# Three more expert-weight buffers, and 23 weight loads issued by GpSimd, in a fused decoder-layer kernel

## The chip, the cores and the metric

The kernel runs on one core of a Trainium2 chip. Its metric is the device time of one launch, in microseconds (us), lower being better; three runs of the kernel before gave 762.72 us in the median (762.62 to 764.26). Five engines work at once, each with its own in-order queue: TensorE (PE, with its weight loads shown as PEld), VectorE (DVE), ScalarE (ACT), GpSimd (POOL) and SyncE (SP, which here issues most transfers). Transfers run on the 16 DMA engines of the core, whoever issues them.

## The reference

One decoder layer on 512 tokens of width 1024, all in float32. A token mixer with three branches, then a mixture of experts:

```
h = rmsnorm(x, g_mix);  proj = h @ w_in          # q, k, v, indexer, conv, memory query, gate logits
o_a = sparse attention: an indexer picks the top 128 causal keys of each query, 8 heads on 2 key heads
o_b = conformer convolution (GLU, causal depthwise conv of 31, layernorm, swish)
o_m = cross-attention to 256 memory tokens
merged = sum over the branches of sigmoid(gate) * (o_branch @ w_br)
x = x + merged @ w_o
h2 = rmsnorm(x, g_ffn)
group = argmax(h2 @ w_rg + b_rg);  two best experts of that group's 8 by h2 @ w_re + b_re
for n in 32 experts: out += combine[:, n] * ((silu(h2 @ up_a[n]) * (h2 @ up_b[n])) @ w_down[n])
x = x + out
```

The weights of the 32 experts are 32 x 3 MB, read once: they are the largest part of the traffic.

## The kernel before, in words

The program has four stretches. The **mixer** (to about 415 us) computes memory keys, convolution, indexer and attention; its weights are 512 KB chunks `w`, loaded on SP into a ring of three buffers (`raw_w`, L130) and split by ACT and DVE into a high part `wh` (L127) and a low part `wl` (L128), which PE multiplies three ways. The **output projection** (the mark "w_o", to about 490 us) multiplies `merged` by w_o in eight column blocks. The **router** (to about 509 us) computes expert choice, token lists and an order of experts. The **experts** run as 16 windows of two experts each (64 tokens an expert) and one further window for the two busiest experts; PE multiplies the gathered tokens `xt` by the expert weights in `up` (L1167) and `down` (L1181).

The expert weights are cut into 192 chunks `we` of 128 x 1024 floats (512 KB, 4 KB a partition). `seq` lists them in the order of use: the first 44 belong to four pairs that are fixed beforehand (EARLY), the later ones to pairs whose numbers DVE works out at run time (`ordi`, L1047) and SP loads into registers (L749). The chunks go round a ring of 42 buffers: `RINGS` says how many buffers each tag has, and the tags lie in memory that other tiles used before (`ot`, `mg`, `wh`, `wl`, `xc`, `hw`, `hx` are tiles of the mixer and of w_o; `w3`, `w1`, `wg`, `s5` lie in pools opened when the mixer's pools `gp` and `bp` are closed). `fetch` (L773) allocates the next buffers of the ring and issues one load each on SP. A load waits until the readers of whatever lay in its buffer are done: for the first turn these are the mixer, w_o or the router, from the second turn on it is the `up` or `down` that used the chunk 42 places earlier. A loaded chunk stays in its buffer until PE has used it.

The instructions of each engine are put in order by a scheduler when the program is built; a row's place can thus move although its code did not. GpSimd computes reciprocal roots (L146, L889), clears tiles, and issues the gathers of tokens (`xg`, L1001), the scatters of results (`out`, L1158) and the reloads of the busiest pair (L1199). [...]

Of the kernel before, what the change touches and what calls it, by code (L numbers as in the profile page):

```python
# [8 lines left out]
F32 = mybir.dt.float32  # L9
# [11 lines left out]
P = 128  # L21
# [19 lines left out]
NPRE = 4  # L41
# [3 lines left out]
def pair(j):  # L45

    e = (j // EPG) * 2 * EPG + j % EPG
    return e, e + EPG


TURN = list(range(NPRE, NW)) + list(range(NPRE))
# [16 lines left out]
for _name, _w in (("g_mix", KD), ("g_mem", KD), ("b_gate", 24), ("conv_b", 4), ("ln_g", 4), ("ln_b", 4),  # L68
# [9 lines left out]
          + [("rkv", i) for i in range(3)] + [(n, i) for n in ("rqi", "rqa") for i in range(4)])  # L78

RING = 3  # L80
RING_A = 9
RING_B = 6
SPLIT = 3
RINGS = (("w3", RING_B), ("w1", RING_A), ("ot", 4), ("mg", 4), ("w", RING), ("wh", SPLIT), ("wl", SPLIT), ("xc", 2),
         ("hw", 3), ("hx", 2), ("wg", 1), ("s5", 2))
CONV_LOW = 1500
TOPK_LOW = 900

# [1 line left out]
def build(nc, tc, I, O, dbg=None):  # L90
    V, A, G, T, SY = nc.vector, nc.scalar, nc.gpsimd, nc.tensor, nc.sync
    es = ExitStack()
    with es:
        cpool = es.enter_context(tc.tile_pool(name="cpool", bufs=1))
        wpool = es.enter_context(tc.tile_pool(name="wpool", bufs=RING))
        spool = es.enter_context(tc.tile_pool(name="spool", bufs=SPLIT))
        mpool = es.enter_context(tc.tile_pool(name="mpool", bufs=1))
# [10 lines left out]
        hp = es.enter_context(tc.tile_pool(name="hp", bufs=1, side="right"))  # L108
        bp = p1b.enter_context(tc.tile_pool(name="bp", bufs=1, side="right"))
        gp = p1a.enter_context(tc.tile_pool(name="gp", bufs=1))  # L110
# [24 lines left out]
        def split_w(w, n=1024):  # L135
            wh = spool.tile([P, 1024], F32R, name="wh", tag="wh")
            wl = spool.tile([P, 1024], F32R, name="wl", tag="wl")
            split_into(wh[:, :n], wl[:, :n], w[:, :n])
            return wh, wl

        def next_w(*key, n=1024):
            return split_w(raw_w(*key), n)
# [55 lines left out]
            return [[hp.tile([P, 2, S], F32R, name=f"{name}{v}{i}", tag="ot", bufs=4) for i in range(2)] for v in "hl"]  # L198

        conv_w = gp.tile([P, 4 * CW], F32, name="conv_wh")  # L200
        bgate = gp.tile([P, 24], F32, name="bgate")
        lng = gp.tile([P, 8], F32, name="lng")
        gqk = gp.tile([P, 1], F32, name="gqk")
        b_r = cpool.tile([P, 36], F32, name="b_r")
# [48 lines left out]
        for k in range(KD):  # L253
# [14 lines left out]
            wh, wl = split_w(kv_raw[k] if k < RING else raw_w("kv", k))  # L268
# [150 lines left out]
        def gate_unit(b, c):  # L419
            ps = mmt("gate")  # L420
            cm_unit(ps, *next_w("gt", b, c))
            t = g2("gt", "gt")
            A.activation(t, ps, AF.Tanh, scale=0.5, bias=bgate[:, b * 8 + c:b * 8 + c + 1])  # L423
            return t
# [31 lines left out]
        for h in range(MH + 1):  # L456
            if h < MH:
                mem_s1(h)
            if h + 1 < MH:
                qm_unit(h + 1)  # L460
            elif len(gm) < 4:
                gm.append(gate_unit(2, len(gm)))
            if h >= 1:
                mem_s2(h - 1)
            if len(gm) < 4 and h > 0:
                gm.append(gate_unit(2, len(gm)))

        mark("A proj")

# [273 lines left out]
        ea = es.enter_context(tc.tile_pool(name="ea", bufs=1, reuse_waits="tile"))  # L743
        rp = es.enter_context(tc.tile_pool(name="rp", bufs=1, side="right", reuse_waits="tile"))
# [7 lines left out]
        def chunk(e, c):  # L752

            if e in EARLY:
                return I["we"][e, c]
            if e not in at_pos:
                at_pos[e] = expert_at(e)
            return I["we"][bass.ds(at_pos[e], 1), c].rearrange("o p n -> (o p) n")
# [3 lines left out]
        for j, last in zip(TURN + [None], [None] + TURN):  # L762
# [3 lines left out]
                seq += [(e, 4 + f) for f in range(2) for e in pair(last)]  # L766
            if j is not None and j != NW:
                seq += [(e, 3) for e in pair(j)]
        pools = dict(ot=hp, hw=hp, hx=hp, w3=rp, xc=rp, w1=ea, w=wpool, wh=spool, wl=spool, s5=ea, wg=ea, mg=mpool)
        slots = [tag for tag, n in RINGS for _ in range(n)]  # L770
        bufs = {tag: slots.count(tag) for tag in slots}
        fetched, used = [], [0]

        def fetch(count, behind=None):
            for n in range(len(fetched), min(len(fetched) + count, len(seq))):
                tag = slots[n % len(slots)]
                w = pools[tag].tile([P, 1024], F32, name="we", tag=tag, bufs=bufs[tag])
                if behind is not None and tag == "s5":
                    G.tensor_copy(w[:, 0:1], behind[:, 0:1])
                e, c = seq[n]  # L780
                SY.dma_start(w, chunk(e, c))  # L781
                fetched.append(w)

        def expert_raw(e, c):
# [8 lines left out]
        def eat(tag, name, bufs=1, dt=F32):  # L793
            return ea.tile([P, 1024], dt, name=name, tag=tag, bufs=bufs)
# [9 lines left out]
        A.dma_start(gB, I["gf"].to_broadcast([P, D]))  # L804
        out_v = O["out"][0:S, :].rearrange("(t p) d -> p t d", p=P)
        h2d_v = h2d.rearrange("(t p) d -> p t d", p=P)
        fetch(RING_B + RING_A + 4 + 4)
        lg = sct("lg")
        zz = eat("s4a", "zz")
        G.memset(zz[:, 0:148], 0.0)  # L810
        T.matmul(lg[:, 0:148], zz[:, 0:P], zz[:, 0:148], start=True, stop=False)
        lists = pvt("lists")

        def back(c, xs):

            ps = trt()
            for t in range(NT):
                T.transpose(ps[:, t * P:(t + 1) * P], xs[:, t * P:(t + 1) * P], ident)
            ys = eat("s5", "x1t", 2)
            if c < KD - 2:  # L820
                A.activation(xs[:, 512:1024], ps, AF.Square)
                V.reduce_sum(sqs[:, :, c], xs[:, 512:1024].rearrange("p (t d) -> p t d", t=NT), axis=AX.X)
            A.copy(ys[:, 0:512], ps)
            g = gB[:, None, c * P:(c + 1) * P].to_broadcast([P, NT, P])
            V.tensor_mul(ys[:, 512:1024].rearrange("p (t d) -> p t d", t=NT), ps.rearrange("p (t d) -> p t d", t=NT), g)
            y3 = ys.rearrange("p (s t d) -> p s t d", s=2, t=NT)
            (SY if c >= KD - 2 else A).dma_start(h2d_v[:, :, c * P:(c + 1) * P], y3[:, 1])
            A.dma_start(out_v[:, :, c * P:(c + 1) * P], y3[:, 0])
# [14 lines left out]
        for c in range(KD):  # L843
            ps = mmt("wo")
            wh, wl = split_w(wo_raw[c])
            for k in range(KD):
                if c >= 1 and k == 4:
                    back(c - 1, logits(c - 1))
                mm3(ps, wh[:, k * P:(k + 1) * P], wl[:, k * P:(k + 1) * P], mgh[k], mgl[k], k == 0, k == KD - 1)
            xs = eat(("s4a", "s4b")[c % 2], "x1c", 1 + c % 2)  # L850
            V.tensor_add(xs[:, 0:512], ps, X[c // 2][:, c % 2])
            if c >= KD - 2:
                A.activation(xs[:, 512:1024], xs[:, 0:512], AF.Square)
            XS[c] = xs
# [3 lines left out]
        xs = logits(KD - 1)  # L858
# [6 lines left out]
                T.matmul(junk, w, x, start=True, stop=True)  # L865

        busy_pe(5, xs[:, 512:1024])
        fetch(RING + 2 * SPLIT + 2)


        mark("router")
# [18 lines left out]
        _, L = r3("lgs", NT, 36)  # L890
# [6 lines left out]
        _, pr = r3("pr", NT, NG)  # L897
# [13 lines left out]
        _, oh = r3("oh", NT, 2, NE)  # L911
# [15 lines left out]
        _, rk = r3("rk", NT, 2, NE)  # L927
# [40 lines left out]
        first = slot_tokens(lists, ea, "f")  # L968
# [255 lines left out]
        AC, AT = {}, {}  # L1224
        fill(0)
        fill(1)
        fetch(len(slots) - len(fetched), first)
        XT[0] = window_x(0)
        order_experts()
        fill(2)  # L1230
# [32 lines left out]
        def extra_windows(j, sl):  # L1263
            ids = [expert_at(e) for e in pair(j)]
            with tc.For_i(0, S // CAP - 1, 1):
                V.tensor_scalar_add(sl, sl, -float(CAP))
                ps = eq.tile([P, 512], F32, name="lists2", tag="tr", bufs=2)
                rb = eat("wg", "soh16o").bitcast(F16)
                one_hot(rb, sl)
                token_lists(ps, rb)  # L1270
                idx = slot_tokens(ps, ea, "o")
                ro = eat("wg", "soh2")
                ps = eq.tile([P, 512], F32, name="scales2", tag="tr", bufs=2)
                one_hot(ro, sl)
                scale_lists(ps, ro)
                lst = (idx,) + slot_scales(ps, ea, "o")
                gather(j, lst[0])
                xt = window_x(j)
                ps = eq.tile([P, 512], F32, name="up", tag="up", bufs=2)

                def chunks(c):
                    ws = []
                    for e in ids:
                        w = rp.tile([P, 1024], F32, name="w3", tag="w3", bufs=RING_B)
                        SY.dma_start(w, I["we"][bass.ds(e, 1), c].rearrange("o p n -> (o p) n"))
                        ws.append(w)
                    return ws

                for c in range(4):
                    up(xt, c, chunks(c), ps)  # L1290
                at = act_t(activate(ps, lst, j), j)
                yp = [eq.tile([P, 512], F32, name=f"dn{n}", tag="dn", bufs=2) for n in range(2)]
                for f in range(2):
                    down(at, f, chunks(4 + f), yp)
                scatter(j, yp, lst[0])
# [108 lines left out]
```

## Time and profile before

| | before |
|---|---|
| median of 3 runs | 762.72 us |
| the profiled execution | 763.3 us |
| its span, first to last instruction | 761.5 us |
| PE / DVE / ACT / POOL busy | 716.2 / 477.2 / 266.1 / 89.0 us |
| `we` chunks loaded on SP | 192 |
| DMA traffic | 161.14 MB |

The span is what the profile covers; 1.8 us of the execution lie around it. A busy time says how long an engine had an instruction in work. PE's is 94% of the span, but its ends are modelled, so it does not tell alone whether PE or what feeds it sets the pace: that is read by stretch, from the share of the DMA engines, from the waits and from the chain that ended last.

### The profile page before, as it was taken

How to read it: one execution, taken by the hardware profiler on the slowest of the kernel's cores; microseconds unless marked ns; L12 is line 12 of the kernel's file. 1: busy time of each engine (PE TensorE's matmuls, PEld its weight loads, DVE VectorE, ACT ScalarE, POOL GpSimd, SP SyncE). 2: the span in 40 equal slices, each digit the busy share in tenths (PEclk: the TensorE clock that was granted, in tenths of full speed). 3: DMA queues.
4: the chain of work that ended last, by engine and by line, in shares of the span. 5: the costliest groups of instructions: out<-in, count | busy, mean ns of one | idle time of the engine just before them, and what ended most of it. 6: DMA issues, size and time to landing. Idle time of an engine off the chain costs nothing. (4 is left out here: it accounts for less than half of the span.)

```text
span 761.5 us, 10081 instructions
## 1 busy us (share of the span) xinstructions
PE 716.2 (94%) x3468; PEld 478.1 (63%) x3468; DVE 477.2 (63%) x1085; ACT 266.1 (35%) x503; POOL 89.0 (12%) x82
## 2 busy tenths in 40 slices
PE   5999999999999999999999999989999998889882
PEld 4778888897878778888777888744333333233220
DVE  5879989999999999999987944272111112111100
ACT  6732254455633366236775432102111111000100
POOL 1010010011000050000000000021236322100010
PEclk9999999999999999999999999999999999999997
DMA  9642221223222221221212899989999999999982
GB/s 355 214 142 83 85 83 55 74 66 111 83 83 83 83 84 64 104 83 52 89 55 96 325 367 350 355 306 379 380 398 357 357 370 384 363 385 396 390 324 48
DMA packets 56685, 161.14 MB, mean 212 GB/s; under 512 B 9508, under 2 KB 17956, under 8 KB 56624
## 3 DMA queue, kind: packets, MB, share of 16 engines
q1 hardware_dynamic: 42320, 147.74, 51.5%
q0 software_dynamic: 6624, 8.46, 4.8%
q10 hardware_dynamic: 7680, 4.20, 1.9%
q8 instruction: 29, 0.48, 0.2%
q14 instruction: 32, 0.26, 0.1%
HBM read 162.93 MB, written 13.11 MB: 231 GB/s over the span
## 5 line engine op out<-in xcount | busy, mean ns | idle before, releaser
L1167 PE MATMUL up<-we,xt 128*64 128x512 f32 x544 | 140.7, 599 | 5.3 <-DMA we<-in_we 5.1
L127 ACT CAST wh<-w 128x1024 fp32r<-128x1024 f32 (+2 forms) x75 | 78.3, 1045 | 81.1 <-PE proj L315 25.4
L128 DVE TENSOR_TENSOR wl<-w,wh 128x1024 fp32r<-128x1024 f32 (+2 forms) x75 | 90.8, 1212 | 13.1 <-ACT wh L127 12.1
L1167 PEld LDWEIGHTS up<-we,xt 128*64 128x64 f32 x544 | 39.1, 136 | 77.3 <-issue 58.1
L329 DVE SCALAR_TENSOR_TENSOR y<-u,conv_wh,y 128x512 f32<-128x512 f32 x120 | 84.1, 743 | 0.3
L1157 DVE COPY y<-dn 128x512 f32<-128x512 f32 x17 | 11.8, 691 | 108.5 <-PE dn L1181 108.5
L1181 PE MATMUL dn<-we,acth 128*64 128x512 f32 x272 | 73.6, 596 | 0.6 <-issue 0.6
L315 PE MATMUL gate<-h,wh 128*128 128x512 f32 x240 | 68.3, 397 | 0.0
L1156 ACT COPY y<-dn 128x512 f32<-128x512 f32 x17 | 10.0, 586 | 123.4 <-PE dn L1181 72.3
L1181 PEld LDWEIGHTS dn<-we,acth 128*64 128x64 f32 x272 | 24.1, 136 | 44.5 <-issue 36.3
L315 PEld LDWEIGHTS gate<-h,wh 128*128 128x128 f32 x240 | 44.4, 188 | 9.4
L1158 POOL DMA_INDIRECT out<-y,midx x16 | 25.4, 1585 | 138.9 <-DVE y L1157 128.8
L315 PE MATMUL gate<-h,wl 128*128 128x512 f32 x120 | 34.8, 400 | 0.0
L315 PE MATMUL mm<-h,wh 128*128 128x512 f32 x120 | 32.6, 396 | 0.0
L1140 ACT COPY xt<-xtr 128x512 f32<-128x512 f32 x18 | 10.4, 585 | 57.7 <-PE xtr L1139 57.6
L423 ACT ACTIVATE gt<-gate,bgate 128x512 f32<-128x512 f32 x24 | 16.5, 686 | 39.8 <-PE gate L315 39.6
L1175 DVE COPY acth<-atr 128x256 f32<-128x256 f32 x17 | 7.2, 424 | 36.7 <-PE atr L1173 36.7
L1150 DVE SCALAR_TENSOR_TENSOR acts<-up,mwt,acts 128x256 f32<-128x256 f32 x16 | 7.7, 483 | 31.8 <-ACT acts L1149 31.8
L605 DVE MAX8 v<-score 128x8 f32<-128x256 f32 (+2 forms) x48 | 26.5, 556 | 0.8
L606 DVE MATCH_REPLACE8 score<-v,score 128x256 f32<-128x256 f32 (+2 forms) x48 | 26.0, 542 | 0.0
L315 PEld LDWEIGHTS gate<-h,wl 128*128 128x128 f32 x120 | 22.5, 188 | 5.5 <-issue 0.5
L315 PEld LDWEIGHTS mm<-h,wh 128*128 128x128 f32 x120 | 22.4, 187 | 5.2
(400 smaller groups left out, 1452.7 us busy)
## 6 DMA issues: line engine op xcount, KB each, us to landing
we<-in_we SPq DMA_DIRECT2D x192, 512.0 KB, 11.3
w<-in_wp SPq DMA_DIRECT2D x75, 512.0 KB, 3.5
x<-in_x SPq DMA_DIRECT2D x4, 512.0 KB, 8.3
xr<-in_xt SPq DMA_DIRECT2D x4, 512.0 KB, 5.2
out<-x1t ACTq DMA_DIRECT2D x8, 256.0 KB, 5.9
h2d<-x1t ACTq DMA_DIRECT2D x6, 256.0 KB, 8.5
m<-in_memt SPq DMA_DIRECT2D x2, 512.0 KB, 5.8
m<-in_mem SPq DMA_DIRECT2D x2, 512.0 KB, 9.7
```

The costliest lines, as they stand in the source:

```text
L127: A.copy(wh, w)
L128: V.tensor_sub(wl, w, wh.bitcast(F32))
L315: T.matmul(ps, a[:, k * P:(k + 1) * P], b[k], start=(a is wh and b is rh and k == 0), stop=(b is rl and k == n - 1))
L329: V.scalar_tensor_tensor(Y[c], U[c][:, j:j + S], w, Y[c], op0=ALU.mult, op1=ALU.add)
L423: A.activation(t, ps, AF.Tanh, scale=0.5, bias=bgate[:, b * 8 + c:b * 8 + c + 1])
L605: V.max(v8, sel[t])
L606: V.match_replace(sel[t], v8, sel[t], GONE)
L1140: (A.copy if i or j == 0 else V.tensor_copy)(xt[i], ps.bitcast(F32))
L1157: V.tensor_copy(y[:, 512:1024], yp[1])
L1158: G.indirect_dma_start(out=O["out"], out_offset=bass.IndirectOffsetOnAxis(ap=ix[:, col:col + 1], axis=0), in_=y, in_offset=None, bounds_ch ...
L1167: T.matmul(ps[h * CAP:(h + 1) * CAP], xt[k // 4][:, o + h * CAP:o + (h + 1) * CAP], ws[h][:, i * 512:(i + 1) * 512], start=(k == 0), stop= ...
L1181: T.matmul(yp[n][h * CAP:(h + 1) * CAP], at[:, f * P + h * CAP:f * P + (h + 1) * CAP], ws[h][:, n * 512:(n + 1) * 512], start=(f == 0), st ...
```

## The change

The DMA scratch area is set to 4 KB a partition, and three buffers of a new tag `wn` are made in the constants' pool. They take the first three chunks, whose loads are issued on SP in the mixer, ahead of the mark "A proj". The ring is now written as a list `SLOTS` of 45 buffers: `wn` 3, `w3` 6, `w1` 6, `wx` 3 (six and three of the former nine `w1`), then as before. The chunks 4 to 26 are issued by GpSimd; three calls of `fetch` replace one, two tiles of w_o's tail (`s4b`, `s5`) are allocated between them so that `w1` lies where the attention's tiles were, and the loads into `ot` and `mg` are preceded by a one-column copy on GpSimd from the 18th chunk's buffer, so that they come behind it. `fetch(AHEAD)` and the last `fetch` are cut to what is left: 10 chunks and 8. The bias tile `bgate` moves to the constants' pool, and the clearing of `zz` from GpSimd to DVE.

```diff
-RING_A = 9
-RING_B = 6
 SPLIT = 3
-RINGS = (("w3", RING_B), ("w1", RING_A), ("ot", 4), ("mg", 4), ("w", RING), ("wh", SPLIT), ("wl", SPLIT), ("xc", 2),
-         ("hw", 3), ("hx", 2), ("wg", 1), ("s5", 2))
+NFREE = 3
+POOLED = 23
+SLOTS = (["wn"] * NFREE + ["w3"] * 6 + ["w1"] * 6 + ["wx"] * 3 + ["ot"] * 4 + ["mg"] * 4
+         + ["w"] * RING + ["wh", "wl", "xc", "wh", "wl", "wh", "wl"]
+         + ["hw"] * 3 + ["hx"] * 2 + ["xc", "wg", "s5", "s5"])
+AHEAD = 10
...
+        first_we = []
+        for i in range(NFREE):
+            w = cpool.tile([P, 1024], F32, name="we", tag="wn", bufs=NFREE)
+            SY.dma_start(w, I["we"][pair(TURN[0])[i % 2], i // 2])
+            first_we.append(w)
+
         mark("A proj")
...
-        fetched, used = [], [0]
+        fetched, used = list(first_we), [0]
...
-                if behind is not None and tag == "s5":
+                if behind is not None and tag in ("ot", "mg", "s5"):
                     G.tensor_copy(w[:, 0:1], behind[:, 0:1])
                 e, c = seq[n]
-                SY.dma_start(w, chunk(e, c))
+                (G if n < NFREE + POOLED else SY).dma_start(w, chunk(e, c))
...
-        fetch(RING_B + RING_A + 4 + 4)
+        fetch(12)
         lg = sct("lg")
         zz = eat("s4a", "zz")
-        G.memset(zz[:, 0:148], 0.0)
+        held = {"s4b": eat("s4b", "x1c", 2), "s5": eat("s5", "x1t", 2)}
+        fetch(3)
+        fetch(POOLED - 15, fetched[-1])
+        V.memset(zz[:, 0:148], 0.0)
...
-        fetch(RING + 2 * SPLIT + 2)
+        fetch(AHEAD)
...
-        fetch(len(slots) - len(fetched), first)
+        fetch(min(len(slots), 2 * (6 * NPRE - 2)) - len(fetched), first)
...
-    nc = bacc.Bacc("TRN2", target_bir_lowering=False, num_devices=1)
+    nc = bacc.Bacc("TRN2", target_bir_lowering=False, num_devices=1, dynamic_dma_scratch_size=4096)
```

How the change moves instructions is seen at three places. On GpSimd, between the mixer's last root (`rc`) and the first gathers, before:

```order
L146 TENSOR_TENSOR rc<-rc,nhalf 128x4
L810 MEMSET zz 128x148
L997 MEMSET xg_4846 128x1024
L997 MEMSET xg_4845 128x1024
L889 TENSOR_TENSOR rsx<-rsx,nhalf 128x4
L1001 DMA xg_4845<-h2d,fidx 128x1024
```

and of the change (its lines stand 2 to 11 lower than those of before):

```order
L148 TENSOR_TENSOR rc<-rc,nhalf 128x4
L789 DMA we<-in_we 128x1024 x15
L1008 MEMSET xg_4858 128x1024
L787 COPY we<-we 128x1 x8
L789 DMA we<-in_we 128x1024 x8
L1008 MEMSET xg_4857 128x1024
L900 TENSOR_TENSOR rsx<-rsx,nhalf 128x4
L1012 DMA xg_4857<-h2d,fidx 128x1024
```

Fifteen loads stand ahead of the first clearing of `xg`, then the eight copies and the other eight loads; the root `rsx` and the gathers follow.

On SP, from the end of w_o to the first chunk whose expert is found at run time, before:

```order
L827 DMA h2d<-x1t 128x4x128
L781 DMA we<-in_we 128x1024 x2
L827 DMA h2d<-x1t 128x4x128
L781 DMA we<-in_we 128x1024 x9
L749 TENSOR_LOAD ordi
L781 ISA
L781 DMA we<-in_we 128x1024
```

and of the change:

```order
L838 DMA h2d<-x1t 128x4x128
L789 DMA we<-in_we 128x1024 x2
L838 DMA h2d<-x1t 128x4x128
L789 DMA we<-in_we 128x1024 x6
L757 TENSOR_LOAD ordi
L789 ISA
L789 DMA we<-in_we 128x1024
```

Six chunk loads instead of nine stand ahead of the load of the expert order; the last two of the nine went into the two buffers that the ring's first chunks leave.

On PE, in the convolution's first block (`mm`) with the transposes of the memory keys (`tr` from `kn`), before:

```order
L315 MATMUL mm<-h_146,wh 128x512
L315 MATMUL mm<-h_147,wh 128x512
L315 MATMUL mm<-hh_137,wl 128x512
L315 MATMUL mm<-hh_139,wl 128x512
L315 MATMUL mm<-hh_141,wl 128x512
L315 MATMUL mm<-h_143,wl 128x512
L315 MATMUL mm<-h_144,wl 128x512
L301 MATMUL tr<-csg,kn_400 128x128 x2
```

and of the change:

```order
L317 MATMUL mm<-h_145,wh 128x512
L317 MATMUL mm<-h_146,wh 128x512
L303 MATMUL tr<-csg,kn_400 128x128 x2
L317 MATMUL mm<-h_147,wh 128x512
L317 MATMUL mm<-hh_137,wl 128x512
```

The first two transposes stand six products earlier, behind seven products of the block.

## Rows read from the trace of the kernel before

**Rows 1.** The chain that ended last: start, us, what.

```profile
727.90 12.45 DMA we<-in_we
...
740.39 1.95 PE up L1167 x6
```

**Rows 2.** Busy time by stretch: engines (x instructions), PE clock, DMA share, GB/s.

```profile
46.00:200.00 154.00, 153.41 (x784) 127.43 (x783) 143.94 (x286) 68.83 (x157) 9.76 (x8) 1.00 0.24 82
...
361.00:415.00 54.00, 53.82 (x264) 41.96 (x263) 47.28 (x136) 39.22 (x83) 0.00 (x0) 1.00 0.19 67
415.00:440.00 25.00, 24.14 (x105) 19.23 (x104) 21.08 (x31) 10.35 (x15) 1.11 (x2) 1.00 0.88 327
440.00:503.00 63.00, 59.65 (x326) 47.67 (x325) 28.43 (x72) 14.57 (x23) 1.96 (x2) 0.99 1.01 363
...
522.00:640.00 118.00, 117.86 (x598) 44.83 (x598) 23.73 (x47) 17.06 (x31) 39.23 (x33) 1.00 1.02 377
640.00:740.00 100.00, 86.04 (x314) 28.32 (x310) 10.96 (x21) 7.79 (x15) 9.92 (x7) 1.00 1.01 380
```

**Rows 3.** The same view, a short stretch where the experts begin.

```profile
511.00:513.00 2.00, 2.00 (x12) 0.71 (x10) 0.00 (x0) 0.00 (x0) 0.00 (x0) 1.00 0.55 148
```

**Rows 4.** What SP's queue waited for, 522 to 740 us: total, times, longest.

```profile
SPq L781 <- DMA we<-in_we: 124.8, 132, 2.8
SPq L781 <- PE up L1167: 6.5, 8, 2.4
```

**Rows 5.** SP's issues from 395 to 511 us: start, us, instruction, count.

```profile
415.15 1.47 SPq L781 DMA_DIRECT2D we<-in_we  x3
423.76 0.33 SPq L132 DMA_DIRECT2D w<-in_wp  x1
...
495.26 11.44 SPq L781 DMA_DIRECT2D we<-in_we  x7
```

**Rows 6.** SP's issues in four further stretches, merged.

```profile
505.90 6.57 SPq L781 DMA_DIRECT2D we<-in_we  x4
...
511.66 2.98 SPq L781 DMA_DIRECT2D we<-in_we  x4
...
532.60 5.42 SPq L781 DMA_DIRECT2D we<-in_we  x5
...
640.54 95.17 SPq L781 DMA_DIRECT2D we<-in_we  x65
```

**Rows 7.** Instructions in order of time, the experts' start, DVE and PE.

```profile
507.46 0.17 DVE L1047 CAST ordi<-order 128x32 int32<-128x32 f32 x1
...
509.70 3.65 PE L1167 MATMUL up<-we,xt 128*64 128x512 f32 x16
```

**Rows 8.** GpSimd in order of time (in brackets: idle before).

```profile
426.86 0.22 POOL L810 MEMSET zz<- 128x148 f32 x1 [136.73 <-DVE mg L450]
...
503.11 1.24 POOL L1001 DMA_INDIRECT xg<-h2d,fidx  x1 [7.86 <-DMA we<-in_we]
```

**Rows 9.** DVE in order of time beside that gather.

```profile
504.09 0.25 DVE L1025 SCALAR_TENSOR_TENSOR gk<-cst,busyf 128x32 f32<-128x32 f32 x1
```

**Rows 10.** ACT's splits in w_o, in order of time.

```profile
435.95 1.05 ACT L127 CAST wh<-w 128x1024 fp32r<-128x1024 f32 x1
```

**Rows 11.** The convolution's first block: PE, GpSimd and DVE in order of time.

```profile
39.50 1.33 PE L315 MATMUL mm<-h,wh 128*128 128x512 f32 x5
...
45.61 0.87 PE L301 MATMUL tr<-csg,kn 128*128 128x128 f32 x6 [0.36 <-DVE kn L293]
...
38.80 1.02 POOL L146 TENSOR_TENSOR kss<-kss,nhalf 128x4 f32<-128x4 f32 x1 [11.01 <-DVE kss L145]
...
40.79 0.67 DVE L293 TENSOR_TENSOR kn<-kv,kss 128x512 f32<-128x512 f32 x1
```

**Rows 12.** The busiest pair's reloads by GpSimd: count, duration ns, first and last start; landing.

```profile
L1199 POOL DMA_INDIRECT we<-in_we,xrow x12: 986/991/1043, 568.9 to 590.6; - x12
...
DMA to landing us min/median/max: 8.2/8.6/9.2
```

More of the change, by code (lines that the diff above doesn't have):

```diff
@@ L200, in build @@
         conv_w = gp.tile([P, 4 * CW], F32, name="conv_wh")
-        bgate = gp.tile([P, 24], F32, name="bgate")
+        bgate = cpool.tile([P, 24], F32, name="bgate")
         lng = gp.tile([P, 8], F32, name="lng")
@@ L768, in build @@
                 seq += [(e, 3) for e in pair(j)]
-        pools = dict(ot=hp, hw=hp, hx=hp, w3=rp, xc=rp, w1=ea, w=wpool, wh=spool, wl=spool, s5=ea, wg=ea, mg=mpool)
-        slots = [tag for tag, n in RINGS for _ in range(n)]
+        pools = dict(wn=cpool, ot=hp, hw=hp, hx=hp, w3=rp, xc=rp, w1=ea, wx=ea, w=wpool, wh=spool, wl=spool, s5=ea, wg=ea, mg=mpool)
+        slots = SLOTS
         bufs = {tag: slots.count(tag) for tag in slots}
-        fetched, used = [], [0]
+        fetched, used = list(first_we), [0]
         def fetch(count, behind=None):
@@ L818, in back @@
                 T.transpose(ps[:, t * P:(t + 1) * P], xs[:, t * P:(t + 1) * P], ident)
-            ys = eat("s5", "x1t", 2)
+            ys = held.pop("s5", None) or eat("s5", "x1t", 2)
             if c < KD - 2:
@@ L849, in build @@
                 mm3(ps, wh[:, k * P:(k + 1) * P], wl[:, k * P:(k + 1) * P], mgh[k], mgl[k], k == 0, k == KD - 1)
-            xs = eat(("s4a", "s4b")[c % 2], "x1c", 1 + c % 2)
+            xs = held.pop("s4b") if c == 1 else eat(("s4a", "s4b")[c % 2], "x1c", 1 + c % 2)
             V.tensor_add(xs[:, 0:512], ps, X[c // 2][:, c % 2])
@@ L1283, in chunks @@
                     for e in ids:
-                        w = rp.tile([P, 1024], F32, name="w3", tag="w3", bufs=RING_B)
+                        w = rp.tile([P, 1024], F32, name="w3", tag="w3", bufs=6)
                         SY.dma_start(w, I["we"][bass.ds(e, 1), c].rearrange("o p n -> (o p) n"))
```

## The prediction

> **What bounds the kernel now.** I read the chain that ended last first. It runs through transfers of expert weights, one behind the other, down to the last, from 727.90 to about 740.35; PE's `up` follows at 740.39 [rows 1]. What ends the kernel is thus the landing of the last of 192 chunks, with a tail of 763.3 - 740.4 = 22.9 us behind it that no edit touches.
>
> Then the busy time by stretch, to see from when this holds [rows 2]. The DMA share is 0.24 in 46:200 and 0.19 in 361:415, 0.88 in 415:440, 1.01 in 440:503, and 1.02 and 1.01 from 522 to 740. PE is full to 640 (117.86 of 118 us) and has room after it (86.04 of 100). So PE starts with a stock of loaded chunks, eats it up, and lives from hand to mouth after that. In between there is a hole: at 511:513 the share is 0.55 [rows 3], because by then the buffers are full.
>
> Third, what SP's chunk loads waited for from 522 on: 124.8 us for earlier transfers of the same kind (its transfers in flight are limited in number) against 6.5 us for PE's `up`, the release of a buffer [rows 4]. The stream is limited by transfers, not by buffers. A buffer more is therefore worth something only once, at the stream's start.
>
> Fourth, SP's issues: 42 chunks in nine rows between 415.15 and 506.7, the first and the last of which are shown [rows 5]; the 43rd comes at 511.66, when PE lets go of the first chunk [rows 6]. PE starts its experts at 509.70 [rows 7], held by a block of stand-in matmuls that ends about 1 us earlier and not by data: the gather issued at 503.11 [rows 8] is answered well before.
>
> **The change part by part.** *Three buffers.* 44 chunks (3 on SP in the mixer, 23 on GpSimd, 18 on SP) can be loaded before PE releases one, and the 45th too: its buffer is free and it needs only `ordi`, written at 507.46 [rows 7], and the register load that SP now reaches three loads earlier. At 511.66 the stream then stands at 45 chunks instead of 42, with PE at the same place; the first load that waits for PE is the 46th, not the 43rd. From there on both kernels run the same steps, one three chunks ahead, so the end comes earlier by three times the stream's pace. Two rows price it. Five issues in 532.60 to 538.02 [rows 6] leave four intervals in 5.42 - 0.33 (one issue, [rows 5]) = 5.09 us: 1.27 us a chunk. And 65 issues in 95.17 us give 1.48 [rows 6], but with the token gathers and result scatters in between, which are bound to windows and not to chunks, and whose number stays. I take 1.27: 3 x 1.27 = **3.8 us** less; 3 x 1.48 = 4.4 is the other end. A further bit of up to 1 us may come from the register load no longer standing between the first reissues (four in 2.98 us where the pace of issue alone is 0.33 each, [rows 6]); I leave it in the range. PE has the room for this: 14 us idle in 640:740 [rows 2].
>
> *Earlier loads.* About seven chunks are issued before 415 now: the three of the mixer, and, by what they wait for, four whose buffers lie where attention tiles end early. This I cost at nothing: whatever is loaded earlier, all buffers are full before 511.66 and the hole [rows 3] only gets longer. The three loads in the mixer lie in a stretch with a share of 0.24 [rows 2]: nothing.
>
> *Loads issued on GpSimd.* Before, it stood idle from the mixer to 426.86 (136.73 us, [rows 8]); that cover takes 15 issues. No row of before has a plain load on GpSimd; the nearest is the gather's issue, 1.24 us, against 0.33 on SP. 23 x 1.24 = 28.5 us. Behind them in its queue stand eight copies that wait for the landing of the 18th chunk, two clearings of `xg`, the root `rsx` and the gathers at 503.11. The loads into `mg` and `ot` wait for w_o's last readers at about 440, and by a gather's duration are issued by 440 + 8 x 1.24 = 450, over 40 us ahead of the gathers: nothing. If that cover went, the gathers, and PE's start with them, would slip by as much.
>
> *w_o's own weights.* They now share the transfers with chunks that GpSimd issues without pause. The load at 423.76 [rows 5] is split by ACT at 435.95 [rows 10], 12.2 us later. With eight chunks ahead of it (its own makes nine) it lands 9 x 1.27 = 11.4 us after its issue: nothing, though only 0.8 us are in hand at that end; with five ahead 4.6 us are.
>
> *Order on PE.* The transposes of `kn` come six products earlier in the first convolution block. `kn` is written at 40.79 to 41.46, behind GpSimd's root that ends at 39.82; PE works on products then [rows 11]. PE would stand there for 0.5 us or so and arrive later at the next transposes, where it stood for `kn` anyway (0.36 us idle ahead of 45.61, [rows 11]). Ends 0 and +0.6; I take 0.
>
> *Smaller scratch.* No row shows what 4 KB hold. GpSimd's densest traffic is the twelve reloads, one per (590.6 - 568.9)/11 = 1.97 us, each landing after 8.6 [rows 12]: 4.4 in flight. As long as that many fit, nothing; I take 0, and keep the other end as a rival. `bgate` and the clearing of `zz` (0.22 us, [rows 8]), now on DVE, which is idle for 3.9 of 25 us there [rows 2], are nothing.
>
> Sum against the profiled execution: 763.3 - 3.8 = 759.5. The median of the runs lies 0.58 below that execution: **758.9 us**.
>
> **The rivals.** *Every earlier load counts.* If the stream could use all its head start, the seven chunks ahead of 415 (8.9 us) and the idle 12% of 415:440 (3.0 us) came out whole: 763.3 - 11.9 = 751.4, as a median 750.8. For it speaks the share of 1.01 from 440 on and a chain that ends in transfers; against it the hole of [rows 3], in which a transfer could have run and found no buffer.
>
> *Hardly any of it counts.* Should the 45th not be in time, and the stretch from 511 to 522 be paced by PE's releases in both kernels, so that the head start shrinks to one chunk by 522: 762.7 - 1.3 = 761.4; with the order on PE at its bad end it is no change at all. For it: 6.5 us of waits for `up` [rows 4]. Against it: a release-paced stream with three more buffers is still three releases ahead.
>
> [...]
>
> *Slower: the scratch holds too little.* With two transfers in flight the reloads take 12 x 8.6/2 = 51.6 us instead of 21.7 [rows 12], and PE's extra window waits for about 30 us: 789. It decides below 4.4 in flight. Nothing speaks for it but that the size is cut.
>
> **How the numbers follow.** The forecast 0.62 (its own range 757.6 to 760.2: 4.4 + 0.9 us less down to 2.5 us), every load counts 0.08, hardly any 0.17, DVE held 0.10, scratch 0.03. What a measurement of this kernel can tell from no change is about 0.2%, 1.5 us: 761.2 to 764.2. So faster 0.62 + 0.08 = 0.70, within 0.2% 0.17, slower 0.13. The range goes from 756.0, which takes in some of a larger gain, to 763.2, which takes in the case of hardly any; the two slow ones and most of the large gain, together 0.2, are left out.
>
> **What would show it.** Right: 45 chunk issues ahead of 511.7 and the first that waits for PE's `up` is the 46th; PE's first expert matmul still within 0.3 us of 509.7; a DMA share near 0 just before 511; the last chunk landing near 736.6, still at the end of the chain, with the same tail of 22.9. Wrong: w_o ending later, with PE waiting for DVE's splits in 415:440 and issues of GpSimd beside them (DVE held); reloads spaced by more than 2 us (scratch); PE waiting for `kn` in the first 50 us by more than 0.6; or transfers no longer at the end of the chain, PE being what is late next.

## The result, and the profile after

The changed kernel takes 757.99 us (median of 4 runs, 757.35 to 758.42) against 763.49 for the kernel before (median of 4); the ratio, estimated from all runs and not from the two medians (0.9928), is 0.9924 (95% interval 0.9901 to 0.9947), that is 5.8 us less (4.0 to 7.6). Forecast were 758.9 us and 3.8 us less, from the three runs of before that were known then; the fourth took 765.44.

Its profiled execution took 757.35 us, with a span of 755.5, 6.0 less than before's. Three landmarks divide each span: PE's first `up` of the experts, the start of the last scatter of results, and the end.

| us | before | after | difference |
|---|---|---|---|
| start of the span to the first `up` | 509.70 | 511.34 | +1.64 |
| first `up` to the last scatter | 239.89 | 234.91 | -4.98 |
| last scatter to the end | 11.92 | 9.25 | -2.67 |

The forecast had 0, -3.8 and 0. The chain that ended last (start, us, what) no longer shows a transfer:

```profile
737.05 1.95 PE up L1178 x6
...
746.53 1.27 POOL out L1169
```

The stand of [rows 1] is reached 3.34 us earlier (737.05 for 740.39). The wait ahead of it is not put down to a chunk any more. PE's last wait for a chunk stands a little earlier (start, us, instruction, in brackets idle before), before:

```profile
732.73 1.93 PE L1167 MATMUL up<-we,xt 128*64 128x512 f32 x6 [1.83 <-DMA we<-in_we]
```

and after:

```profile
729.43 1.93 PE L1178 MATMUL up<-we,xt 128*64 128x512 f32 x6 [1.90 <-DMA we<-in_we]
```

It ends 3.30 us earlier, and from there PE works without a gap to 738.99. So the stream still sets the pace, if only just, as the busy times by stretch show too (columns as in [rows 2]):

```profile
361.00:415.00 54.00, 53.84 (x265) 42.01 (x264) 47.86 (x140) 40.76 (x85) 2.44 (x4) 1.00 0.31 108
415.00:440.00 25.00, 24.14 (x104) 19.16 (x103) 20.89 (x32) 10.25 (x15) 6.84 (x12) 1.00 0.92 357
440.00:503.00 63.00, 59.62 (x316) 48.20 (x314) 28.30 (x69) 14.75 (x24) 7.91 (x18) 1.00 0.89 308
...
511.00:513.00 2.00, 2.00 (x24) 0.89 (x25) 0.36 (x2) 0.78 (x2) 1.01 (x1) 1.00 0.85 274
...
522.00:640.00 118.00, 118.00 (x640) 44.81 (x638) 23.11 (x48) 16.47 (x30) 38.25 (x32) 1.00 1.02 380
640.00:736.00 96.00, 81.86 (x321) 28.03 (x318) 11.79 (x21) 8.13 (x16) 10.96 (x8) 1.00 1.01 380
```

The DMA share is 1.02 and 1.01 from 522 on, as before [rows 2]. The head start is in the first rows (0.31 for 0.19 in 361:415), and it is given back as forecast: 0.89 for 1.01 in 440:503. In 415:440 PE and DVE are as busy as before (24.14 and 20.89 us) with twelve GpSimd instructions beside them. At 511:513 the share is 0.85 for 0.55 [rows 3], but PE's first `up` comes 1.64 us later here. At the same distance behind it the hole is still there, a little shallower and not longer:

```profile
512.64:514.64 2.00, 2.00 (x12) 0.71 (x10) 0.00 (x0) 0.00 (x0) 0.00 (x0) 1.00 0.66 182
```

SP's waits from 522 to 737 are of the kind of [rows 4]:

```profile
SPq L789 <- DMA we<-in_we: 118.6, 128, 3.1
SPq L789 <- PE up L1178: 5.4, 6, 2.1
```

By the starts and landings in before's trace, 133 of SP's 140 chunk loads from 522 to 740 are the eighth of SP's in flight when they are issued, the other seven the sixth or seventh, and none the ninth: the limit in number behind [rows 4].

### The profile page after: what moved, and what is told of

It is laid out like the page before. It is cut to its first block, busy times and chain, and to the rows that moved or that the text cites. A ratio compares the mean times of both kernels' runs of the same rounds, so it can differ in the third digit from the quotient of the medians.

```text
span 755.5 us, 10093 instructions
## 1 busy us (share of the span) xinstructions
PE 713.0 (94%) x3468; PEld 476.4 (63%) x3468; DVE 477.4 (63%) x1086; ACT 266.1 (35%) x503; POOL 108.4 (14%) x111
## 5 line engine op out<-in xcount | busy, mean ns | idle before, releaser
L1178 PE MATMUL up<-we,xt 128*64 128x512 f32 x544 | 136.7, 599 | 4.4 <-DMA we<-in_we 4.3
L1192 PE MATMUL dn<-we,acth 128*64 128x512 f32 x272 | 71.9, 596 | 0.6 <-issue 0.6
L789 POOL DMA_DIRECT2D we<-in_we x23 | 12.5, 550 | 126.6 <-ACT oah L724 72.2
```

The lines of the kernel that those rows point to most:

```text
L789: (G if n < NFREE + POOLED else SY).dma_start(w, chunk(e, c))
L1178: T.matmul(ps[h * CAP:(h + 1) * CAP], xt[k // 4][:, o + h * CAP:o + (h + 1) * CAP], ws[h][:, i * 512:(i + 1) * 512], start=(k == 0), stop= ...
L1192: T.matmul(yp[n][h * CAP:(h + 1) * CAP], at[:, f * P + h * CAP:f * P + (h + 1) * CAP], ws[h][:, n * 512:(n + 1) * 512], start=(f == 0), st ...
```

## The experiments

Eleven runs, in three sets. Behind each profile stand its landmarks, from the same records as above:

| run | buffers | scratch | first `up` | to last scatter | to the end | ratio to before |
|---|---|---|---|---|---|---|
| before | 42 | default | 509.70 | 239.89 | 11.92 | 1 |
| scratch_16k | 42 | 16 KB | 510.69 | 239.35 | 12.00 | one run, 763.88 us |
| scratch_8k | 42 | 8 KB | 512.68 | 239.98 | 10.11 | 0.9977 (0.9965 to 0.9988) |
| scratch_only | 42 | 4 KB | 510.15 | 240.44 | 9.47 | 0.9964 (0.9951 to 0.9978) |
| scratch_1k | 42 | 1 KB | 510.64 | 239.69 | 8.10 | 0.9943 (0.9929 to 0.9956) |
| pool_only | 42 | 4 KB | 512.19 | 239.41 | 9.49 | 0.9955 (0.9938 to 0.9971) |
| nfree1 | 43 | 4 KB | 510.35 | 237.91 | 9.50 | 0.9932 (0.9919 to 0.9945) |
| buffers_only | 45 | 4 KB | 510.93 | 235.54 | 9.39 | 0.9920 (0.9897 to 0.9943) |
| after | 45 | 4 KB | 511.34 | 234.91 | 9.25 | 0.9924 (0.9901 to 0.9947) |
| after_again | 45 | 4 KB | 510.80 | 235.01 | 9.61 | 0.9910 (0.9887 to 0.9934) |
| four_1k | 46 | 1 KB | 511.46 | 233.47 | 8.08 | 0.9866 (0.9851 to 0.9880) |
| four_1k_again | 46 | 1 KB | 510.05 | 234.34 | 8.80 | 0.9888 (0.9869 to 0.9906) |
| four_sp | 46 | 1 KB | 510.58 | 234.83 | 8.11 | 0.9900 (0.9882 to 0.9917) |

**First set: what each part is worth.** *scratch_only* is the kernel before with one word more.

```diff
-    nc = bacc.Bacc("TRN2", target_bir_lowering=False, num_devices=1)
+    nc = bacc.Bacc("TRN2", target_bir_lowering=False, num_devices=1, dynamic_dma_scratch_size=4096)
```

> The kernel before with its DMA scratch cut to 4 KB and nothing else: 42 buffers, all chunk loads on SP, the same order of instructions. If the smaller scratch holds enough: ratio to before 1.000 (within 0.2%), the twelve reloads still one per 1.97 us. If it holds too little: reloads spaced wider and up to 30 us more. It also repeats before's order in another execution: if the length of GpSimd's roots in the mixer is set by the order, the root at 173.6 lasts 1.75 us again and the experts start at 509.7 again; if it varies by chance, it doesn't. Likewise the time from the last scatter's issue to the span's end (11.9 us in before's profile, 9.25 in that of the change): by chance if it differs here.

It is faster, 0.9964, about 2.7 us (1.7 to 3.7), which neither reading had. The reloads keep their pace (569.3 to 591.2 for twelve, 1.99 us each), so the smaller scratch does not hold them up; the gain lies behind the last scatter, 9.47 us for 11.92. The root at 174.15 lasts 1.75 us as in before, yet the experts start at 510.15 and not at 509.7.

*buffers_only* adds to that three buffers at the head of the ring, all loads on SP:

```diff
-RINGS = (("w3", RING_B), ("w1", RING_A), ...
+RINGS = (("wn", 3), ("w3", RING_B), ("w1", RING_A), ...
...
-        fetch(RING_B + RING_A + 4 + 4)
+        fetch(3 + RING_B + RING_A + 4 + 4)
...
-        fetch(len(slots) - len(fetched), first)
+        fetch(min(len(slots), 2 * (6 * NPRE - 2)) - len(fetched), first)
```

> Three more buffers from a 4 KB scratch, put first in the ring; all loads on SP from 415 us on, none earlier, none on GpSimd. Theory (three buffers are worth three chunks of the saturated stream): 3.8 us less than before at the last chunk's landing, and the whole gain of the change. The tile pool's new tag shifts PE's order in the first convolution block as the full change does, so if that order causes the late start of the experts (+1.6 us), it is here too, and the net is about that of the change, -3.5 us. Rival (the head start on GpSimd and in the mixer counts): under 1.5 us less than before.

0.9920, the whole size of the change, without one load on GpSimd. From the first `up` to the last scatter it takes 235.54 us, 4.3 less than the mean of the six kernels with 42 buffers (239.8).

It is not without early loads, though none was expected. The three new buffers are free from the start, and the scheduler put their loads into the mixer here too, where the change has them by its text (30.22, 35.70 and 36.17 us there):

```profile
30.09 0.43 SPq L781 DMA_DIRECT2D we<-in_we  x1
35.96 0.90 SPq L781 DMA_DIRECT2D we<-in_we  x2
...
416.37 1.69 SPq L781 DMA_DIRECT2D we<-in_we  x3
```

What the run leaves out are the four loads that GpSimd issues ahead of 415 us, and its others. Every kernel here with extra buffers loads as many chunks in the mixer as it has extra buffers; that the buffers would be worth as much with all loads from 415 us on is not shown. There was room for it: by before's shares, 0.88 in 415:440 [rows 2] and 0.75 in the row below, some 3.5 and 2.3 us of transfer time lay idle below the 1.02 of the later stretches, an estimate, and three chunks want 3.8.

```profile
503.00:511.66 8.66, 8.66 (x55) 4.09 (x55) 6.47 (x45) 1.07 (x2) 3.61 (x5) 0.87 0.75 253
```

*pool_only* is the change with `NFREE = 0`.

> The change without its three buffers: 42 buffers, 23 loads on GpSimd, 4 KB scratch, the order of the first block as before. Theory (buffers alone count): 0 against before, experts' start at 509.7, last chunk at 740.3. Rival (earlier loads count): up to 8 us less. [...] If the late start of the change comes from the order in the first block, the roots on GpSimd are as long as before here.

0.9955 can't be told from the scratch alone (0.9964). The middle stretch, 239.41, is at the low edge of what 42 buffers give (239.35 to 240.44). With 42 buffers the head start (four chunks ahead of 415 us, and the quicker issues behind them) is worth nothing that these runs can measure. w_o isn't held up: PE waits there for the same two things as in before, 0.9 and 0.8 us.

*after_again* is the change once more.

> The change once more, for its size on the same chip and for a second profile. If order sets the roots' length, the root at 174.15 us lasts 5.6 us again, the experts start at 511.3 again and the last chunk lands at 737.0; if it is chance, the start is anywhere from 509.7 to 511.3. From the last scatter's issue to the end: 9.25 us again, or up to 11.9 if that part varies by chance. Ratio to before 0.993 to 0.995.

The middle and the end repeat (235.01 and 9.61 us), and the ratio, 0.9910 (0.9887 to 0.9934), is a little below the expected. The start does not repeat: 510.80 for 511.34, and GpSimd's fourth root there lasts 1.75 us where it lasted 5.58 (below, with the other profiles).

**Second set: the scratch's size, and the price of a buffer.** *scratch_1k* and *scratch_8k* are scratch_only with 1024 and 8192.

> The kernel before with a 1 KB scratch and nothing else. Theory (GpSimd's closing drain grows with the scratch: 3.82 us with the size of before, 1.69 with 4 KB): if that size is four times 4 KB and the drain is linear in it, 0.18 us a KB, so 1.2 us here, and with its neighbour, 1.11 and 0.59 us, 0.5: about 0.7 us less than with 4 KB, 3.4 us less than before. Rival (too small a scratch holds up transfers): the twelve reloads spaced by more than 1.97 us, and the kernel slower than with 4 KB.

> The kernel before with an 8 KB scratch and nothing else. Theory (drain linear in the scratch): 2.4 us of drain, its neighbour 0.76, so 1.8 us less than before. Rival (the drain has two levels, or differs by chance): 3.8 or 1.7 us.

Both sizes came out where the closing drain was expected, or below. The rows of the program's last line in the three sizes (queue, instruction and count, shortest, middle and longest in ns, first and last start); the longest is the one that counts. With 8 KB:

```profile
L1400 POOLq DRAIN  x3: 46/107/2347, 759.6 to 762.5; - x3
```

with 4 KB:

```profile
L1400 POOLq DRAIN  x3: 46/107/1693, 757.5 to 759.8; - x3
```

and with 1 KB:

```profile
L1400 POOLq DRAIN  x3: 46/107/468, 756.9 to 758.1; - x3
```

An instruction of GpSimd just ahead of it shrinks along, 0.75, 0.59 and 0.29 us. Together that is 3.10, 2.28 and 0.76 us, for 4.93 before: 1.8, 2.65 and 4.2 us less. The timed ratios say 1.8, 2.7 and 4.4 us (of 765). Below 4 KB the drain falls faster than the line said (0.47 for 1.2 us).

*nfree1* is the change with `NFREE = 1`, *four_1k* the change with `NFREE = 4` and 1 KB.

> The change with one extra buffer instead of three (4 KB scratch, 24 early loads). Theory (each buffer is worth one chunk of the stream): from the experts' start to the last chunk's landing 2 x 1.27 = 2.5 us longer than in the change, 1.3 shorter than without the three; ratio to before about 0.9945. Rival (the loads on GpSimd, or the first load's place, make the gain): as the change, within 0.5 us.

> The change with a fourth extra buffer, for which the scratch goes to 1 KB. Theory: one chunk more, 1.27 us, and 0.7 us of the closing drain: 2 us less than the change, ratio to before about 0.989. Rival (1 KB is too little for 23 loads with eight in flight): issues on GpSimd from 417 on wider apart than 0.54 us, w_o or the reloads late, no gain.

One buffer shortens the middle stretch by 1.9 us against the mean of 239.8, three by 4.6 (mean of 235.54, 234.91 and 235.01), four by 6.3, 5.4 and 5.0 (the two profiles of four_1k and that of four_sp, below). That is 1.2 to 1.9 us a buffer, by three buffers 1.55. GpSimd's later issues in four_1k (start, us, instruction, in brackets idle before), with 1 KB:

```profile
441.95 4.24 POOL L789 DMA_DIRECT2D we<-in_we  x7
447.23 0.54 POOL L789 DMA_DIRECT2D we<-in_we  x1 [1.05 <-issue]
```

The change with 4 KB has the eight together in 4.24 us. Here seven take that long, 0.62 us apart and not 0.53, and the eighth is held up by another 1.05 us (1.95 in four_1k_again); nobody waits for it. So the rival was right about the issues and wrong about the time. four_1k takes 754.99 us, 10.2 less than before on the same chip, and beats both kernels. By the landmarks the fourth buffer and the smaller scratch take 1.4 and 1.2 us off the change, for 1.3 and 0.7 expected.

**Third set: the shortest version.** *four_sp* is buffers_only with 4 for 3 and 1 KB; *four_1k_again* stands beside it; *scratch_16k* is scratch_only with 16384.

> Four extra buffers and a 1 KB scratch alone: all loads on SP, none before 415 us. Theory (buffers and scratch make the whole gain; each buffer 1.6 us from the experts' start to the last scatter, as nfree1 and the change showed, and the closing part 8.1 us): 239.9 - 4 x 1.6 = 233.5 us for that stretch and the same time as the version with the loads on GpSimd, within 0.15%. Rival (the loads on GpSimd and in the mixer are worth something by themselves): slower than that version by 0.5 us or more in that stretch.

> The change with four extra buffers and a 1 KB scratch again, beside four_sp on the same chip: 233.5 us from the experts' start to the last scatter, 8.1 us behind it, ratio to before 0.987. The experts' start itself is expected anywhere from 509.7 to 512.7, by chance.

> The kernel before with a scratch of 16 KB written out. If that is the size that it has anyway: the closing drain lasts 3.8 us and its neighbour 1.1 us, as before; from the last scatter to the end 11.9 us. By the line through 4 and 8 KB (1.69 and 2.35 us, 0.165 us a KB) the drain would be 3.7 us.

four_sp has 755.41 us and four_1k_again 754.84, 0.08% apart, with intervals that overlap. In the middle stretch four_sp is 0.5 and 1.4 us slower than the two profiles of its rival, buffers_only 0.5 and 0.6 slower than the change: all in one direction, and 0.5 is what the rival asked for, yet all but the 1.4 are within what kernels with 42 buffers differ by among themselves (1.1), and the two profiles of four_1k's kernel differ by 0.9. Both stay above the 233.5 us that were expected. Whether the loads on GpSimd bring some tenths in that stretch stays open; in the time of the kernel no difference shows. scratch_16k has before's drain and its neighbour again to the nanosecond (3817 and 1108), so the default behaves as 16 KB:

```profile
L1400 POOLq DRAIN  x3: 46/107/3817, 757.4 to 761.8; - x3
```

## Why the prediction was right, point by point

**Three buffers: right in mechanism, too small in size.** The first load that waits for PE is the 46th: it is issued 1.96 us after the first `up` (513.30 and 511.34), nearly where before's 43rd stood [rows 6, 7] (511.66 and 509.70). SP's row of it (start, us, instruction):

```profile
513.30 0.34 SPq L789 DMA_DIRECT2D we<-in_we  x1
```

All thirteen profiles have this: the first load that finds no free buffer is the 43rd, 44th, 46th or 47th with 42, 43, 45 or 46 buffers, and comes 1.94 or 1.96 us after the first `up`. From then on the stream is three chunks further than before's. The term was 3 x 1.27 = 3.8 us; measured are 4.6 (mean of three profiles), 1.55 a chunk. The other end of the bound, 1.48 a chunk and 4.4 us, was the nearer. The reason for leaving it out, that gathers and scatters go with the windows and not with the chunks, may not hold for the start: in the first 12.3 us from the first `up` the transfers are busier in the changed kernel. Before (columns as in [rows 2]):

```profile
509.70:522.00 12.30, 12.30 (x132) 6.05 (x131) 3.24 (x11) 2.78 (x4) 1.93 (x2) 1.00 0.85 295
```

and after:

```profile
511.34:523.64 12.30, 12.30 (x132) 6.05 (x131) 3.23 (x11) 2.78 (x4) 1.93 (x2) 1.00 0.90 314
```

0.05 of 12.3 us is 0.6 us of transfer time that before lost there. It could be part of the missing 1.2 in this pair (4.98 for 3.8), but that share also varies among the kernels with 42 buffers (0.85 in before, 0.94 in scratch_only), so where it comes from is not settled. The further bit of up to 1 us, from the register load, is about 0.3: four reissues span 2.30 us from the first start to the last (513.30 to 515.60) for 2.64 before (511.66 to 514.30). Beside this term the lower end of the forecast's own range is a slip: 4.4 + 0.9 us less than 762.7 are 757.4, not 757.6.

**The scratch: the step that failed.** The prediction set the smaller scratch at nothing, with losses as the other end, and wrote that the tail of 22.9 us is touched by no edit. It looked for the cost where GpSimd's transfers run and not at the program's end, where a drain grows with the scratch (3.82 us with 16 KB, 1.69 with 4). That the small scratch costs nothing as long as 4.4 reloads in flight fit was the author's estimate; no run shows how many it holds, and in scratch_1k the twelve still start 2.02 us apart (570.0 to 592.2), for 1.97 in before. By itself the smaller scratch is a gain of 2.7 us, as much as 1.7 buffers. In the change, with 23 loads more on GpSimd, the drain and its neighbour last 1.83 and 0.63 us: 2.46 for 4.93 before, most of the 2.67 us that the end is shorter by. In this pair of profiles the forecast's 759.5 becomes 759.5 - 2.7 (scratch) - 1.2 (buffers) + 1.6 (later start) = 757.2, for 757.35 measured: two gains that were missed, and a loss by chance that hid most of one. That the number came out so near is in part luck.

**The later start: chance, not the change.** The transposes of `kn` do cost PE 0.59 us, as forecast (0.5 or so), and the next ones wait 0.51 for 0.36. Rows of PE after:

```profile
40.36 0.41 PE L303 MATMUL tr<-csg,kn 128*128 128x128 f32 x2 [0.59 <-DVE kn L295]
45.72 0.87 PE L303 MATMUL tr<-csg,kn 128*128 128x128 f32 x6 [0.51 <-DVE kn L295]
```

PE is 0.1 us late behind them. Most of the rest arises at 165 to 180 us, where GpSimd's reciprocal roots run beside DVE: 0.5 us at the first, which lasts 0.95 us in before and 1.43 in the other twelve profiles, and 0.75 at the fourth. The fourth, before, after, and in after_again:

```profile
173.56 1.75 POOL L146 TENSOR_TENSOR kss<-kss,nhalf 128x3 f32<-128x3 f32 x1 [1.21 <-DVE kss L145]
```

```profile
174.15 5.58 POOL L148 TENSOR_TENSOR kss<-kss,nhalf 128x3 f32<-128x3 f32 x1 [1.21 <-DVE kss L147]
```

```profile
175.15 1.75 POOL L148 TENSOR_TENSOR kss<-kss,nhalf 128x3 f32<-128x3 f32 x1 [1.21 <-DVE kss L147]
```

The last two are the same kernel. Over the thirteen profiles the fourth root is long in seven, three with the order of before on PE and four with that of the change, and short in the other six, three with either order. DVE after, behind the last instruction that it has ready:

```profile
177.81 1.21 DVE L130 TENSOR_TENSOR wl<-w,wh 128x1024 fp32r<-128x1024 f32 x1
179.76 0.36 DVE L540 TENSOR_TENSOR kr<-kr,kss 128x192 f32<-128x192 f32 x1 [0.74 <-POOL kss L148]
```

DVE falls idle at 179.02 and the root of 174.15 ends at 179.73. In after_again the short root is over at 176.90, with the same instructions of DVE beside it (weight splits from 174.98 and 177.50). What decides between the two lengths is not shown. Kernels with the order of before on PE start their experts between 509.70 and 512.68, those with the order of the change between 510.05 and 511.46 (table): the order costs nothing that shows, and before's profile happened to be the earliest of all.

**Loads on GpSimd: nothing, as forecast.** The price was bounded by a gather's issue, 1.24 us. The rows of GpSimd after:

```profile
417.05 4.28 POOL L789 DMA_DIRECT2D we<-in_we  x8 [8.29 <-PE pva L716]
```

Eight in 4.28 us are 0.54 each: the eleven issues in 415:440 take 5.9 us, where 1.24 each would be 13.6. That they hold up DVE, the 0.10 among the chances, was the author's estimate, and the runs do not show it. DVE's busy time in 415:440 is 20.89 for 21.08. Before, an instruction of DVE ran its 0.25 us within a gather's issue of 1.24 [rows 8, 9]; after, DVE splits a weight in its usual 1.22 us while GpSimd issues a load within it:

```profile
424.12 1.22 DVE L130 TENSOR_TENSOR wl<-w,wh 128x1024 fp32r<-128x1024 f32 x1
```

```profile
424.84 0.54 POOL L789 DMA_DIRECT2D we<-in_we  x1 [0.74 <-DMA we<-in_we]
```

**Signs that did not come.** A DMA share near 0 just before 511 was expected, with all buffers full; it is 0.75 in 510:511. SP's waits in 495:512 show why it isn't:

```profile
SPq L789 <- POOL we L787: 4.7, 1, 4.7
SPq L789 <- DVE slot L940: 3.3, 1, 3.3
```

The 44th chunk goes behind a one-column copy on GpSimd, which now stands behind the gathers, and is issued at 507.36 where 505.9 was expected; the 45th follows at 510.04. Both still come ahead of PE's first release, and that is all that counts here. PE's first `up` was to be within 0.3 us of 509.7 and came at 511.34, by chance as said. The last chunk was to stand at the end of the chain, with the same tail of 22.9 us: the tail is 757.35 - 737.05 = 20.3 us, by the drain, and the chain no longer reaches a transfer. That was named as a sign of being wrong, with PE late next, and it came in part: PE has no gap from 729.43 to the last chunk's products. But one buffer more still pays: the kernels with four are 5.0 to 6.3 us below the mean of 239.8 where those with three are 4.3 to 4.9.

**The rivals.** Every earlier load counts: fell, pool_only gives no more than the scratch. Hardly any of it counts: fell, 4.6 us in the middle stretch. DVE held: not seen. Scratch too small: fell in time, even at 1 KB, where the issues are held up a little.

## What to carry to other kernels

When a stream of transfers sets the end, count in buffers, and price one at the stream's all-in pace with everything that shares it (measured 1.55 us a buffer here, 1.27 were forecast); loads that start earlier, without more buffers, made no measurable difference here (0.9955 for 0.9964). A setting that is cut for the sake of something else can change a time of its own: here the program's closing drain fell from 3.82 to 1.69 us as the scratch went from 16 to 4 KB, so look at the very end too. And before reading a microsecond off one pair of profiles, look at how far the same landmark moves between executions of one kernel.

## What the runs showed of the hardware

- GpSimd's last drain grows with its DMA scratch: 0.47, 1.69, 2.35 and 3.82 us at 1, 4, 8 and 16 KB. The times of whole kernels follow (0.9943, 0.9964, 0.9977 of before at 1, 4 and 8 KB). With 23 loads more on GpSimd it is a little longer, 0.48 and 1.83 us at 1 and 4 KB.
- A root of three columns on GpSimd lasts either 1.75 or 5.58 us at the same place of the same program (5.57 or 5.58 in seven of thirteen profiles), and moves what follows by 0.8 us (PE's offset between before and after goes from 0.6 to 1.4 us across it).
- A plain 512 KB load costs 0.54 us of issue on GpSimd (0.77 and 0.60 for its first two) and 0.33 on SP, 0.4 to 0.5 mostly where several stand in a row. With a 1 KB scratch seven on GpSimd go out 0.62 us apart, for 0.53 with 4 KB, and the eighth waits 1.05 or 1.95 us more.
